# Nineteen second-pass pairs by seven products instead of fourteen, sums of their weights on GpSimd, ten units kept unrounded

## The chip, the cores and the metric

The kernel runs on one core of one Trainium2 chip. The metric is the device time of one execution in microseconds (us); the kernel before takes 2128.05 us in the median of three runs (2127.59 to 2128.74). The engines of the core work side by side, each through its own queue in order: TensorE (PE, matrix products), VectorE (DVE), ScalarE (ACT), GpSimd (POOL) and SyncE (SP, whose queue issues most loads). GpSimd's queue also issues loads and stores.

## What is computed

Two layers of a decoder, 256 tokens by 2048 features, all in float32. The part that the change touches is the second half of each layer:

```python
hm = _rmsnorm(x, mlp_norm_g[l]) @ w_up[l]          # 256x2048 by 2048x8192
x = x + jnp.square(jax.nn.relu(hm)) @ w_down[l]    # 256x8192 by 8192x2048
```

A float32 product is made of three products of rounded operands: each operand is split into hi (rounded) and lo (the rest), and hi*hi, hi*lo and lo*hi are added up (TERMS). ScalarE writes hi as a rounded copy, VectorE writes lo as a subtraction, source minus hi.

## The kernel before

The 8192 hidden features are worked through as 32 **pairs** of 128 features (NP = 32). A pair's activations are a block of two by two (two halves of the tokens, two groups of features), and so is a half of its rows of w_down: two groups of 128 rows by two column chunks of 512 (CH).

- **First pass** (`for i in range(NP)`, from line 1176): the up projection of pair i (L1124, results named upc), its square (`square`, L1137), and, two pairs later (LAG = 2), the product with the left 1024 columns of w_down, by seven products in place of eight block products (L1172, results named pr). The seven products need sums of the activations (S1 to S4, a **unit** h of eight 128x128 blocks, VectorE in `square`) and sums of the weights (t, four 128x512 blocks). `rounded` (L1161) splits a unit into hi and lo (f). The units are stored to DRAM for the second pass: as all seven rounded blocks (`whole`, 896 KB) for pairs that go by seven again, as four rounded blocks (`plain`) for the others. L1250 then does the left columns of the last two pairs.
- **Second pass** (`for i in ORDER`, L1274): the right 1024 columns of w_down, in the order 30, 31, 0, 1, ..., 29 (ORDER). Results are named rt. Fourteen pairs (SEVEN: every second one from the fourth on) go by seven products: seven times three terms, 21 matmuls of 128x512 (L1172 again). The other eighteen (ORDINARY) go by eight block products, 24 matmuls (L1337; the last at L1322). Their activations come back from DRAM through GpSimd's queue (`load_unit`, L1078): f for a seven, g (two pairs a block, `block`) for an ordinary one.
- **Weights** are made by jobs. An ordinary pair has two: a raw tile is loaded, and each of its halves is split into whi and wlo (L325 on ScalarE, L326 on VectorE, 128x1024). A seven has three (`quarters`, L989): plain (b1 of 128x512 and b2 of 128x1024), sums (t13) and more (t24), each split by L998 (ScalarE) and L999 (VectorE). The sums themselves are three VectorE operations: t[0:2] of 128x1024 (L1016), t[2] and t[3] of 128x512 (L1019, L1020). `weights.take` makes jobs three ahead of the one that TensorE uses (AHEAD = 3); in the second pass a table (`weights.order`) spreads a seven's three jobs between those of the ordinary pairs ahead of it.
- **Order**: TensorE's instructions are in program order. A scheduler orders the other engines' instructions, except that those marked `late` keep their program order, and those issued within `behind(x)` come after x. Tiles of a pool share buffers: an instruction that writes a tile waits until the buffer's last user is done.

Each layer begins with the mixer (attention, gated convolution, output projection, whose results are named q, k, v, gc, ci, gb, o). GpSimd does some elementwise work there, such as scaling the gate (L841) and the convolution's result (L736), and the small factors of the norms (L501, L708, L711).

Of the kernel before, what the change touches and what calls it, by code (L numbers as in the profile page):

```python
# [15 lines left out]
P = 128  # L16
# [96 lines left out]
def trunk(ctx: ExitStack, tc: tile.TileContext, x, w_in, w_out, conv_w, q_norm_g, k_norm_g,  # L113
# [5 lines left out]
    xpool = ctx.enter_context(tc.tile_pool(name="xpool", bufs=1))  # L119
    apool = ctx.enter_context(tc.tile_pool(name="apool", bufs=4))  # L120
    wpool = ctx.enter_context(tc.tile_pool(name="wpool", bufs=3))
# [382 lines left out]
    class Norm:  # L504
# [3 lines left out]
        def __init__(self, which, l):  # L508
            self.which, self.l = which, l
            self.squared = 0  # L510
            self.tiles = [Parts(apool, "a", f"nT{which}{l}_{n}") for n in range(D // CH)]
            self.ss = small.tile([P, NT, D // CH], F32, tag="ss", name=f"ss{which}{l}", bufs=2)
# [253 lines left out]
    def mixer(l, norm, loads):  # L766

        with ExitStack() as scope:
# [23 lines left out]

            def part_rooms():
                return (apool.tile([P, 2, 2 * CH], F32, tag="a", name="oraw"),
                        apool.tile([P, 4, CH], F32, tag="a", name="ot"))

            load_seven = {}
            for i in SIDE:
                if i in SIDE_SEVEN:
                    load_seven[i] = weights.seven(  # L800
                        w_out[l], 2 * P * i, bias_room if i == SIDE_SEVEN[0] else part_rooms,
                        spare2)
# [130 lines left out]
    def mlp(l, mnorm, ahead, last):  # L933
# [3 lines left out]
        with ExitStack() as scope:  # L937
            upool = scope.enter_context(tc.tile_pool(name="upool", bufs=3))
            fpool = scope.enter_context(tc.tile_pool(name="fpool", bufs=2))
# [21 lines left out]
            def column(i, c, kh):  # L961
                def make():
                    if c == 0:
                        raws[kh] = upool.tile([P, 8, 2 * P], F32, tag="uraw", name="uraw")
# [12 lines left out]
                weights.jobs.append(make)  # L977

            def load_rows(i, col):
                raw = (upool.tile([P, 2, 2 * CH], F32, tag="uraw", name="raw") if col and i not in SEVEN else  # L980
                       tile_of("draw", [P, 2, 2 * CH], F32, (first, "draw"), (second, "draw1"),
                               (second, "draw2")))
# [6 lines left out]
            def quarters(i, col=0):  # L989


                keep = late if i == SEVEN[0] and col else lambda ins: None

                def parts(src, tag, bufs):
                    hi, lo = (tile_of(tag + p, list(src.shape), F32R,
                                      *((r, tag + p) for r in (quarter if tag[0] == "b" else halves, second)[:bufs]))
                              for p in "hl")
                    keep(nc.scalar.activation(hi, src, AF.Copy))  # L998
                    keep(nc.vector.tensor_sub(lo, src, hi.bitcast(F32)))  # L999
                    return hi, lo  # L1000

                def load():
                    forms["raw"] = load_rows(i, col).rearrange("p k (n c) -> p k n c", n=2)
                    return forms["raw"]

                def plain():
                    raw = forms["raw"] if i == col == 0 else load()
                    h1, l1 = parts(raw[:, 0, 0], "b1", 2)
# [3 lines left out]
                def sums():  # L1012
                    raw = forms["raw"]
                    t = forms["t"] = first.tile([P, 4, CH], F32, tag="t", name="t")

                    keep(nc.vector.tensor_sub(t[:, 0:2], raw[:, :, 1], raw[:, 0]))  # L1016
                    h, lw = parts(t[:, 0:2], "t13", 1)

                    keep(nc.vector.tensor_add(t[:, 2], t[:, 1], raw[:, 0, 0]))  # L1019
                    keep(nc.vector.tensor_sub(t[:, 3], raw[:, 1, 0], t[:, 2]))  # L1020
                    return (h[:, 0], lw[:, 0]), (h[:, 1], lw[:, 1])
# [4 lines left out]

                if i == 0 and col == 0:
                    made = {}
# [4 lines left out]
                    return tuple(lambda n=n: made[n] for n in range(3))  # L1033
                if i == 1 and not col:

# [5 lines left out]
                    return tuple(behind_last(make) for make in (plain, sums, more))  # L1041
                return plain, sums, more

            def rows(i, k, box, col=0):
# [19 lines left out]
            for i in range(NP - LAG, NP):  # L1064
# [5 lines left out]

            whole = {i: dram.tile([P, 2, 7, P], F32R, name=f"whole{l}_{i}") for i in SEVEN}
            plain = [dram.tile([P, 2, 2, 4, P], F32R, name=f"plain{l}_{b}")
                     for b in range(len(PLAIN) // 2)]
            again, unit_loads = {}, []

            def load_unit(dst, src):
                with behind(*unit_loads[-1:]):
                    unit_loads.append(nc.gpsimd.dma_start(dst, src))  # L1078

            def load_again(i):  # L1080
                again[i] = fpool.tile([P, 2, 8, P], F32R, tag="f", name="f")
                load_unit(again[i][:, :, 1:], whole[i])

            base = len(weights.jobs)
            where = {}
            for i in ORDER:
                where[i] = len(weights.jobs)
                if i in SEVEN:
                    weights.jobs += quarters(i, 2 * CH)
# [4 lines left out]
            made_in = list(range(base))  # L1094
            mine = [where[i] + k for i in ORDINARY for k in range(2)]
            slots = {}
            for i in SEVEN:
                before = [j for j in mine if j < where[i]][-4:] if i != SEVEN[0] else [
                    mine[0], mine[1], mine[4]]
                js = [where[i] + k for k in range(3)]  # L1100
                if len(before) == 4 and SEVEN.index(i) and where[SEVEN[SEVEN.index(i) - 1]] > before[0]:
                    before = [before[2], before[2], before[3]]
                for j, b in zip(js, before):
                    slots.setdefault(b, []).append(j)
            for j in mine:
                made_in.append(j)
                made_in += slots.get(j, [])
            weights.order = made_in

# [27 lines left out]
            def square(i, h):  # L1137
# [8 lines left out]
                if i < NP - LAG:  # L1146
# [73 lines left out]
            def block(b):  # L1220
                blocks[b] = apool.tile([P, 2, 2, 4, P], F32R, tag="a", name="g")
                for s in range(2):
                    load_unit(blocks[b][:, s], plain[b][:, s])
# [48 lines left out]
            for n in (5, 4, 8):  # L1272
                prods[n] = bank(f"rt{l}{n}")
            for i in ORDER:  # L1274
                if i in SEVEN:
# [27 lines left out]
                n = ORDINARY.index(i)  # L1303
                if NP // 2 - 6 <= n and sums:
                    finish_left()
                if 0 < n <= len(SEVEN):
                    load_again(SEVEN[n - 1])
                b, slot = divmod(n - LAG, 2)
# [79 lines left out]
```

## Time and profile before

| what | before |
|---|---|
| median of three runs | 2128.05 us (2127.59 to 2128.74) |
| the profiled execution, whole | 2129.09 us |
| its span, first to last instruction | 2127.1 us |
| granted TensorE clock | 1.00 throughout |
| up projection and first pass, layer 0 | about 392 to 902 us |
| second pass, layer 0 | 902.2 to 1067.6 us |
| up projection and first pass, layer 1 | about 1448 to 1958 us |
| ScalarE, VectorE, GpSimd busy | 61%, 81%, 9% of the span |

In the profile's rows L12 is line 12 of the kernel, "out<-in" names the tiles, "xcount" the number of instructions, and an arrow "<-" behind an idle time names what ended the wait. "Busy" time of an engine includes time that an instruction spends held up after it has started. Matmul durations overlap, so TensorE's rate is read from the chain of waits, whose pieces follow one another.

### The profile page before, as it was taken

Reading aid. Unit: us, or ns where it says so; the run is one execution under the profiler, and the core shown is the slowest. Engines: PE = TensorE matmul, PEld = TensorE weight load, DVE = VectorE, ACT = ScalarE, POOL = GpSimd, SP = SyncE. Lnnn points to the kernel's source line nnn. Section 1 sums busy time; section 2 is a strip of 40 time slices with the busy share of each in tenths; the row PEclk is TensorE's granted clock in tenths of the full one; section 3 lists DMA queues with packets and bytes.
Section 4 is the critical chain, followed back from the end, with each engine's and each line's share of the span. In section 5 each row is a group of like instructions: output and inputs, shape, how many; then the busy total and the mean of one; then the engine's idle time right before and its main releaser. Section 6 shows DMA issues by size and latency. Waiting matters only on the chain.

```text
span 2127.1 us, 28890 instructions
## 1 busy us (share of the span) xinstructions
PE 2121.4 (100%) x10932; PEld 1806.0 (85%) x10932; DVE 1727.1 (81%) x2379; ACT 1295.3 (61%) x1771; POOL 188.9 (9%) x282
## 2 busy tenths in 40 slices
PE   9999999999999999999999999999999999999999
PEld 7888888888888888888888888888888888888887
DVE  6677678788888888799866776887888888887897
ACT  6556456666666666555565664566666666665553
POOL 2021200000000000011011221000000000000110
PEclk9999999999999999999999999999999999999999
DMA  7655567687777777699666556676778778786994
GB/s 249 199 159 168 179 218 244 205 253 243 241 246 243 242 246 243 215 363 345 224 210 178 159 167 192 212 249 218 239 245 250 236 245 250 236 246 209 385 357 158
DMA packets 293322, 497.99 MB, mean 234 GB/s; under 512 B 10723, under 2 KB 191541, under 8 KB 293184
## 3 DMA queue, kind: packets, MB, share of 16 engines
q1 hardware_dynamic: 263056, 406.88, 60.0%
q0 software_dynamic: 30080, 89.26, 13.0%
q8 instruction: 85, 1.39, 0.3%
q14 instruction: 53, 0.43, 0.1%
q10 hardware_dynamic: 48, 0.02, 0.0%
HBM read 451.53 MB, written 44.59 MB: 233 GB/s over the span
## 4 chain that ended last, share of the span: by engine, by line
PE 99%; DVE 0%; DMA 0%; ACT 0%; issue 0%
PE upc L1124 31%; PE pr L1172 14%; PE rt L1337 8%; PE rt L1172 6%; PE ci L479 4%; PE gc L479 4%; PE gb L479 4%; PE q L457 4%; PE k L457 4%; PE v L457 4%; PE o L457 4%; PE o L875 3%; PE o L893 1%; PE upw L1124 1%; PE up L1124 1%; PE pr L1250 1%
## 5 line engine op out<-in xcount | busy, mean ns | idle before, releaser
L325 ACT ACTIVATE whi<-raw 128x1024 fp32r<-128x1024 f32 x308 | 326.4, 1060 | 407.9 <-PE rt L1337 138.7
L326 DVE TENSOR_TENSOR wlo<-raw,whi 128x1024 fp32r<-128x1024 f32 x308 | 378.6, 1231 | 196.6 <-ACT whi L325 191.6
L1124 PE MATMUL upc<-nT,uhi 128*128 128x512 f32 x1920 | 477.5, 391 | 0.0
L974 ACT ACTIVATE uhi<-uraw 128x1024 fp32r<-128x1024 f32 x256 | 270.5, 1057 | 262.9 <-PE upc L1124 238.6
L975 DVE TENSOR_TENSOR ulo<-uraw,uhi 128x1024 fp32r<-128x1024 f32 x256 | 313.0, 1223 | 123.5 <-ACT uhi L974 113.8
L1124 PEld LDWEIGHTS upc<-nT,uhi 128*128 128x128 f32 x1920 | 352.7, 188 | 68.2
L1124 PEld LDWEIGHTS upc<-nT,ulo 128*128 128x128 f32 x1920 | 261.9, 190 | 18.7
L1124 PE MATMUL upc<-nT,ulo 128*128 128x256 f32 x1920 | 267.7, 282 | 0.0
L1337 PE MATMUL rt<-whi,g 128*128 128x512 f32 x480 | 152.8, 389 | 0.0
L999 DVE TENSOR_TENSOR t13l<-t,t13h 128x1024 fp32r<-128x1024 f32 x88 | 107.5, 1222 | 1.8
L1016 DVE TENSOR_TENSOR t<-draw 128x1024 f32<-128x1024 f32 x88 | 107.3, 1220 | 0.8
L999 DVE TENSOR_TENSOR t24l<-t,t24h 128x1024 fp32r<-128x1024 f32 x88 | 107.1, 1217 | 0.0
L999 DVE TENSOR_TENSOR b2l<-draw,b2h 128x1024 fp32r<-128x1024 f32 x88 | 107.1, 1217 | 0.0
L1337 PEld LDWEIGHTS rt<-whi,g 128*128 128x128 f32 x480 | 90.1, 188 | 18.6
L998 ACT ACTIVATE t13h<-t 128x1024 fp32r<-128x1024 f32 x88 | 93.4, 1061 | 3.0 <-PE rt L1172 0.6
L1172 PE MATMUL pr<-t13h,f 128*128 128x512 f32 x240 | 93.8, 391 | 0.0
L1337 PE MATMUL rt<-wlo,g 128*128 128x512 f32 x240 | 93.4, 389 | 0.0
L998 ACT ACTIVATE b2h<-draw 128x1024 fp32r<-128x1024 f32 x88 | 92.4, 1050 | 0.9 <-PE pr L1172 0.8
L998 ACT ACTIVATE t24h<-t 128x1024 fp32r<-128x1024 f32 x88 | 92.7, 1053 | 0.2
L457 PE MATMUL k<-whi,nT 128*128 128x512 f32 x256 | 86.1, 400 | 0.0
L457 PE MATMUL q<-whi,nT 128*128 128x512 f32 x256 | 84.8, 401 | 0.0
L457 PE MATMUL v<-whi,nT 128*128 128x512 f32 x256 | 84.1, 396 | 0.0
(414 smaller groups left out, 4097.2 us busy)
## 6 DMA issues: line engine op xcount, KB each, us to landing
uraw<-in_w_up_dram SPq DMA_DIRECT2D x128, 1024.0 KB, 5.8
raw<-in_w_in_dram SPq DMA_DIRECT2D x190, 512.0 KB, 4.1
draw<-in_w_down_dram SPq DMA_DIRECT2D x92, 1024.0 KB, 6.5
raw<-in_w_down_dram SPq DMA_DIRECT2D x36, 1024.0 KB, 8.2
raw<-in_w_out_dram SPq DMA_DIRECT2D x52, 512.0 KB, 4.6
whole<-f POOLq DMA_DIRECT2D x28, 896.0 KB, 4.5
f<-whole POOLq DMA_DIRECT2D x28, 896.0 KB, 8.6
plain<-f POOLq DMA_DIRECT2D x32, 512.0 KB, 3.7
```

What stands on the lines that cost most here:

```text
L325: self.splits.append((nc.scalar.activation(hi, raw, AF.Copy), nc.vector.tensor_sub(lo, raw, hi.bitcast(F32))))
L326: nc.vector.tensor_sub(lo, raw, hi.bitcast(F32))))
L457: nc.tensor.matmul(acc[:, t], a.ap[:, pa, k % KG, t * P:(t + 1) * P], (hi, lo)[pw][:, j], start=(k == 0 and n == 0), stop=(k == nk - 1 and ...
L479: nc.tensor.matmul(acc[:, f, 0] if part else acc[:, f], wt[:, k % 4, fs], a.ap[:, 0, k % KG] if part else a.ap[:, :, k % KG], start=(part ...
L974: nc.scalar.activation(hi, src, AF.Copy)
L975: nc.vector.tensor_sub(lo, src, hi.bitcast(F32))
L998: keep(nc.scalar.activation(hi, src, AF.Copy))
L999: keep(nc.vector.tensor_sub(lo, src, hi.bitcast(F32)))
L1016: keep(nc.vector.tensor_sub(t[:, 0:2], raw[:, :, 1], raw[:, 0]))
L1124: nc.tensor.matmul(acc[:, 0] if part else acc, wt[:, k], a.ap[:, 0, k % KG] if part else a.ap[:, :, k % KG], start=(part == 0 and kh == 0 ...
L1172: nc.tensor.matmul(prods[n], f[:, pa, a], b[pw], start=(start and m == 0), stop=(stop and m == 2))
L1337: nc.tensor.matmul(prods[p], own(k, t, pa), w[pw][:, n], start=(i == ORDER[0] and k == 0 and m == 0), stop=False)
```

## The change

Nineteen pairs of the second pass go by seven products: in positions 3, 4, 6, 7, 9, 10, ... 27, 28 of ORDER, and 29. Thirteen stay ordinary. A steady piece of the second pass is now ordinary, seven, seven.

Ten of the nineteen (KEPT: those whose position is not divisible by three) have their unit stored as four unrounded blocks in place of seven rounded ones. In the second pass the four come back, GpSimd makes S1 to S4 again (`unit_again`, four operations of 128x128, L1147), and ScalarE and VectorE round the unit again (L1217, L1218, 128x896).

The weights' sums of the second pass are now three GpSimd operations (`right_sums`, L1065 to L1067) made two pairs ahead, marked `late`; the loads are issued three pairs ahead (`right_load`). The splits are L1075 (ScalarE) and L1076 (VectorE), into forms that take turns over five rooms (`form_room`). The table of the second pass's jobs is gone: jobs are made in ORDER, three ahead. The pools apool and upool give each tile a buffer of its own name. In the first pass the sums stay on VectorE.

```diff
-SEVEN = ORDER[3:NP - LAG:2]
+SEVEN = tuple(i for p, i in enumerate(ORDER[:NP - LAG]) if p > LAG and p % 3 < 2 or p == NP - LAG - 1)
+KEPT = tuple(i for p, i in enumerate(ORDER) if i in SEVEN and p % 3)
...
+            def right_sums(n):
+                if n >= len(SEVEN):
+                    return
+                raw = raws[n, "r"]
+                t = raws[n, "t"] = tile_of("t", [P, 4, CH], F32, (upool, "u2"), (first, "t"))
+                late(nc.gpsimd.tensor_tensor(t[:, 0:2], raw[:, :, 1], raw[:, 0], op=ALU.subtract))
+                late(nc.gpsimd.tensor_tensor(t[:, 2], t[:, 1], raw[:, 0, 0], op=ALU.add))
+                late(nc.gpsimd.tensor_tensor(t[:, 3], raw[:, 1, 0], t[:, 2], op=ALU.subtract))
...
+            def right_jobs(n):
...
+                def plain():
+                    raw = raws[n, "r"]
+                    b1 = parts(raw[:, 0, 0], [
+                        tile_of("b1" + p, [P, CH], F32R, (quarter, "b1" + p), (second, "b1" + p))
+                        for p in "hl"])
+                    h, lw = parts(raw[:, 1], form_room())
+                    return b1, (h[:, 0], lw[:, 0]), (h[:, 1], lw[:, 1])
...
+            def unit_again(n):
...
+                if i in KEPT:
+                    h = again[n, "h"]
+                    for dst, x, y, op in ((S1, A21, A22, ALU.add), (S2, S1, A11, ALU.subtract),
+                                          (S3, A11, A21, ALU.subtract), (S4, A12, S2, ALU.subtract)):
+                        late(nc.gpsimd.tensor_tensor(h[:, dst], h[:, x], h[:, y], op=op))
+                    again[i] = rounded(h, 1, 8)
+                else:
+                    again[i] = fpool.tile([P, 2, 8, P], F32R, tag="f", name="f")
+                    load_unit(again[i][:, :, 1:], whole[i])
...
                 if i in SEVEN:
+                    if i in KEPT:
+                        stored.append(nc.gpsimd.dma_start(kept[i], h[:, 0:4]))
                     f = rounded(h, 1, 8)
-                    nc.gpsimd.dma_start(whole[i], f[:, :, 1:])
+                    if i not in KEPT:
+                        nc.gpsimd.dma_start(whole[i], f[:, :, 1:])
...
                     product(4, f, A22, t4, False)
                     work.tick()
+                    n = SEVEN.index(i)
+                    right_load(n + 3)
+                    load_kept(n + 3)
+                    right_sums(n + 2)
+                    unit_again(n + 2)
```

GpSimd's queue in the middle of layer 0's second pass, first before the change (f and g are units loaded back; in brackets what a row waits for: PE, DVE, Pool and Activation are the engines, DMASW a transfer of GpSimd's queue, DMAHW one of SP's):

```order
L1078 DMA f<-whole_7_3825 128x2x896 [waits DMASW7_49,DMASW1_49,PE_49]
L1078 DMA f<-whole_9_3826 128x2x896 [waits DMASW4_49,PE_49]
L1078 DMA g<-plain_3_3839 128x1024
L1078 DMA g<-plain_3_3839 128x1024 [waits DMASW2_49]
L1078 DMA f<-whole_11_3827 128x2x896 [waits DMASW7_49,DMASW3_49,PE_49]
```

And the same place with the change, one period of three pairs (t are sums of weights, h the unit of a kept pair, draw the raw weights):

```order
L1131 DMA h<-kept_8_3833 128x512
L1065 TENSOR_TENSOR t<-draw 128x1024 [waits DMAHW6_49,DVE_49]
L1066 TENSOR_TENSOR t<-t,draw 128x512 [waits Pool_49]
L1067 TENSOR_TENSOR t<-draw,t 128x512 [waits Pool_49]
L1131 DMA f<-whole_7_3824 128x2x896 [waits DMASW5_49,PE_49]
L1065 TENSOR_TENSOR t<-draw 128x1024 [waits DMAHW0_49,DVE_49]
L1066 TENSOR_TENSOR t<-t,draw 128x512 [waits Pool_49]
L1067 TENSOR_TENSOR t<-draw,t 128x512 [waits Pool_49]
L1147 TENSOR_TENSOR h<-h 128x128 [waits DMASW0_49]
L1147 TENSOR_TENSOR h<-h 128x128 [waits Pool_49]
L1147 TENSOR_TENSOR h<-h 128x128
L1147 TENSOR_TENSOR h<-h 128x128 [waits Pool_49]
```

Loads alone have become loads with ten elementwise operations between them in each period; the load of a rounded unit (f) waits for TensorE and stands ahead of the second pair's sums.

VectorE's queue in layer 0's second pass before the change, one ordinary pair and one seven (wlo, t24l, b1l, b2l and t13l are lo parts, t the sums):

```order
L326 TENSOR_TENSOR wlo<-raw,whi 128x1024
L999 TENSOR_TENSOR t24l<-t,t24h 128x1024
L999 TENSOR_TENSOR b1l<-draw,b1h 128x512
L999 TENSOR_TENSOR b2l<-draw,b2h 128x1024
L999 TENSOR_TENSOR t13l<-t,t13h 128x1024
L1016 TENSOR_TENSOR t<-draw 128x1024
L1019 TENSOR_TENSOR t<-t,draw 128x512
L326 TENSOR_TENSOR wlo<-raw,whi 128x1024
L1020 TENSOR_TENSOR t<-draw,t 128x512
```

With the change, one ordinary pair and two sevens (wfl and wf are lo parts of the forms, f a kept unit's lo part, x an addition of results):

```order
L327 TENSOR_TENSOR wlo<-raw,whi 128x1024
L1320 TENSOR_TENSOR x_83<-x_83,e_8501 128x512
L1218 TENSOR_TENSOR f<-h,f 128x896
L327 TENSOR_TENSOR wlo<-raw,whi 128x1024
L1076 TENSOR_TENSOR b1l<-draw,b1h 128x512
L1076 TENSOR_TENSOR wfl<-t,wfh 128x1024
L1076 TENSOR_TENSOR wfl<-draw,wfh 128x1024
L1076 TENSOR_TENSOR wfl<-t,wfh 128x1024
L1076 TENSOR_TENSOR b1l<-draw,b1h 128x512
L1076 TENSOR_TENSOR wfl<-t,wfh 128x1024
L1076 TENSOR_TENSOR wf<-draw,wf 128x1024
L1076 TENSOR_TENSOR wfl<-t,wfh 128x1024
```

The three sums have left VectorE's queue, and the rounding of a kept unit has come in.

More of the change, by code (lines that the diff above doesn't have):

```diff
@@ L979, in load_rows @@
             def load_rows(i, col):
-                raw = (upool.tile([P, 2, 2 * CH], F32, tag="uraw", name="raw") if col and i not in SEVEN else
+                raw = (tile_of("raw", [P, 2, 2 * CH], F32, (upool, "u0"), (upool, "u1"))
+                       if col and i not in SEVEN else
                        tile_of("draw", [P, 2, 2 * CH], F32, (first, "draw"), (second, "draw1"),
@@ L987, in load_rows, with quarters @@
                 return raw
-            def quarters(i, col=0):
-                keep = late if i == SEVEN[0] and col else lambda ins: None
+            def quarters(i):
                 def parts(src, tag, bufs):
@@ L1067, in mlp @@
                 rows(i, 1, box)
-            whole = {i: dram.tile([P, 2, 7, P], F32R, name=f"whole{l}_{i}") for i in SEVEN}
+            whole = {i: dram.tile([P, 2, 7, P], F32R, name=f"whole{l}_{i}")
+                     for i in SEVEN if i not in KEPT}
+            kept = {i: dram.tile([P, 4, P], F32, name=f"kept{l}_{i}") for i in KEPT}
             plain = [dram.tile([P, 2, 2, 4, P], F32R, name=f"plain{l}_{b}")
-                     for b in range(len(PLAIN) // 2)]
+                     for b in range((len(PLAIN) + 1) // 2)]
             again, unit_loads = {}, []
@@ L1078, in load_unit, with load_kept @@
                     unit_loads.append(nc.gpsimd.dma_start(dst, src))
[L1080 to L1085, printed above, removed]
+                late(unit_loads[-1])
+            def load_kept(n):
+                if n < len(SEVEN) and SEVEN[n] in KEPT:
+                    h = again[n, "h"] = tile_of("h", [P, 8, P], F32, (fpool, "h"), (second, "h"))
+                    load_unit(h[:, 0:4], kept[SEVEN[n]])
+            def unit_again(n):
+                if n >= len(SEVEN):
+                    return
+                i = SEVEN[n]
+                if i in KEPT:
[7 more added lines that the diff above has]
+                    load_unit(again[i][:, :, 1:], whole[i])
             for i in ORDER:
-                where[i] = len(weights.jobs)
                 if i in SEVEN:
-                    weights.jobs += quarters(i, 2 * CH)
+                    weights.jobs += right_jobs(SEVEN.index(i))
                 else:
@@ L1093, in mlp @@
                     rows(i, 1, box, 2 * CH)
[L1094 to L1108, printed above, removed]
             def column_bank():
@@ L1273, in mlp @@
                 prods[n] = bank(f"rt{l}{n}")
+            for n in range(3):
+                right_load(n)
             for i in ORDER:
```

73 lines of the change are left out of this document (51 added, 22 removed).

## The prediction

> **What bounds the kernel now.** I read the page first, then the chain of waits at the first layer's second pass, then the stages, then VectorE's and GpSimd's groups, then single overlaps in the timeline.
>
> ```profile
> span 2127.1 us, 28890 instructions
> PE 2121.4 (100%) x10932; PEld 1806.0 (85%) x10932; DVE 1727.1 (81%) x2379; ACT 1295.3 (61%) x1771; POOL 188.9 (9%) x282
> PE 99%; DVE 0%; DMA 0%; ACT 0%; issue 0%
> ```
>
> TensorE is busy throughout and is 99% of the chain that ended last. So a matmul removed is time gained, as long as nothing else becomes late. GpSimd, at 9%, looks free.
>
> ```profile
> 883.65 5.56 PE upc L1124 x32
> 889.21 2.07 PE pr L1172 x9
> 891.28 10.88 PE pr L1250 x48
> 902.16 16.32 PE rt L1337 x72
> 918.48 4.76 PE rt L1172 x21
> 923.24 5.44 PE rt L1337 x24
> ...
> 1062.17 5.44 PE rt L1322 x24
> ```
>
> This is the chain (start, length, what) around the second pass of layer 0. L1337 is an ordinary pair, L1172 a pair by seven products. A pair of 24 matmuls takes 5.44 us, one of 21 takes 4.76: 0.2267 us per matmul. The pass runs without a gap from 902.16 to 1062.17 + 5.44 = 1067.61 us. Layer 1 repeats it.
>
> ```profile
> core 0: us, PE busy (x) PEld busy (x) DVE busy (x) ACT busy (x) POOL busy (x), PEclk, DMA share, GB/s
> 891.00:1069.00 178.00, 178.00 (x799) 147.67 (x798) 155.32 (x166) 97.61 (x117) 17.60 (x28) 1.00 0.83 294
> ```
>
> In that stage VectorE is busy 155.3 of 178 us, and GpSimd does nothing but issue 28 loads. VectorE is the next bound there; the change takes work from it and gives it to GpSimd.
>
> **What is removed.** Five more pairs per layer go from 24 to 21 matmuls: 5 x 3 x 2 = 30 matmuls, 30 x 0.2267 = 6.80 us. If everything else stays hidden, the profiled execution goes from 2129.09 (its span of 2127.1 and 2.0 around it) to 2122.29 us. The median of the runs is 2128.05, 1.04 under the profiled one, so that case is 2121.2.
>
> **What VectorE has to do per period.** In the steady part three pairs repeat: one ordinary, one seven with a stored rounded unit, one seven with a kept unit. TensorE needs 66 x 0.2267 = 14.96 us for them.
>
> ```profile
> L326 DVE TENSOR_TENSOR wlo<-raw,whi 128x1024 fp32r<-128x1024 f32 x37 | 45.2, 1224 | 18.0 <-ACT whi L325 17.9
> L1016 DVE TENSOR_TENSOR t<-draw 128x1024 f32<-128x1024 f32 x14 | 17.1, 1223 | 0.4
> L999 DVE TENSOR_TENSOR b1l<-draw,b1h 128x512 fp32r<-128x512 f32 x14 | 9.6, 685 | 0.0
> L1019 DVE TENSOR_TENSOR t<-t,draw 128x512 f32<-128x512 f32 x14 | 9.6, 688 | 0.3
> ```
>
> These are groups of the same stage (busy us, mean ns). An ordinary pair has two lo parts of 128x1024 (L326): 2.44 us. A seven has three of them and a 128x512 one: 3 x 1.22 + 0.69 = 4.35 us. The sums (1.22 + 2 x 0.69 = 2.60 us a pair, L1016 to L1020) leave VectorE. A kept unit adds one rounding of 128x896, by elements 7/8 of 1.22 = 1.07 us. Sum: 2.44 + 2 x 4.35 + 1.07 = 12.2 us. That is under 14.96: alone, VectorE would have become more comfortable than it was. ScalarE makes the hi parts to the same shapes; priced like VectorE's they are 5 x (4.35 - 2.44) + 10 x 1.07 = 20 us more on top of its 98 of 178 us, so it has room.
>
> **What GpSimd has to do per period.**
>
> ```profile
> L841 POOL TENSOR_TENSOR gc02w<-gc02w,rowb 128x512 f32<-128x512 f32 x1 | 1.3, 1287 | 0.0
> L708 POOL TENSOR_TENSOR ams<-ams,rc x32: 195/197/654, 111.5 to 1281.2; 128x2 f32<-128x2 f32 x32
> L1078 POOL DMA_DIRECT2D f<-whole x14 | 10.0, 712 | 131.3 <-PE rt L1172 106.2 <-PE rt L1337 25.1
> L1078 POOL DMA_DIRECT2D g<-plain x14 | 7.7, 551 | 0.0
> ```
>
> A 128x512 operation took 1.29 us, a 128x2 one 0.195 us (shortest and median). The 128x1024 one of the change does not occur in this trace: at most two of 512, 2.58 us; at least twice the 1.15 us that a 512 one takes once it runs (below), 2.30 us. A 128x128 one lies between a quarter of 1.15 (0.29) and the line through the two rows (0.47). Sums of a pair: 4.60 to 5.16 us. Sums of a kept unit, four operations: 1.16 to 1.88. Per period 2 x 4.60 + 1.16 = 10.4 to 12.2 us, and about three DMA issues of 0.55 to 0.71. GpSimd alone would fit into 14.96, if barely. The Trainium skill ("GPSIMD Engine Reference", Performance versus the Vector engine) gives 4497 ns for 2048 elements; an estimate from it is 2.25 us for 1024, and the sum of a pair would be 4.55 us. No run here shows that size yet.
>
> **Where the two meet.** The timeline of the mixer stage shows GpSimd beside VectorE:
>
> ```profile
> 226.49 1.29 POOL L841 TENSOR_TENSOR gc02w<-gc02w,rowb 128x512 f32<-128x512 f32 x1
> 226.70 2.15 DVE L326 TENSOR_TENSOR wlo<-raw,whi 128x1024 fp32r<-128x1024 f32 x1 [0.97 <-ACT whi L325]
> 227.73 1.18 POOL L711 TENSOR_TENSOR af<-a_r,rc 128x2 f32<-128x2 f32 x1
> ...
> 1319.20 1.22 DVE L326 TENSOR_TENSOR wlo<-raw,whi 128x1024 fp32r<-128x1024 f32 x1
> 1319.30 2.27 POOL L736 TENSOR_TENSOR cv<-cv,rowb 128x512 f32<-128x512 f32 x1 [13.72 <-ACT whi L325]
> ...
> 248.37 1.29 POOL L841 TENSOR_TENSOR gc03w<-gc03w,rowb 128x512 f32<-128x512 f32 x1 [5.06 <-DVE gc03w L493]
> 249.26 1.49 DVE L326 TENSOR_TENSOR wlo<-raw,whi 128x1024 fp32r<-128x1024 f32 x1 [0.97 <-ACT whi L325]
> ...
> 200.68 1.29 POOL L841 TENSOR_TENSOR gc01w<-gc01w,rowb 128x512 f32<-128x512 f32 x1
> 201.22 0.56 DVE L686 TENSOR_TENSOR pT<-ptp,pT 128x384 fp32r<-128x384 f32 x1 [1.30 <-ACT pT L685]
> ```
>
> VectorE's subtraction that started at 226.70 took 2.15 us, not 1.22: it ended 1.07 us after GpSimd's operation did (226.49 + 1.29 = 227.78). The tiny GpSimd operation behind it, worth 0.2, took 1.18 and ended with VectorE's, at 228.9. At 1319.30 GpSimd took 2.27, ending 1.15 us after VectorE's end. At 249.26 VectorE ended 1.09 us after GpSimd. In each of these cases one waited for the whole of the other. At 201.22 a VectorE operation with one source in PSUM (ptp) ran beside GpSimd at its usual 0.56. So two operands in SBUF on both sides exclude each other. All the VectorE work counted above (L327, L1076 and L1218 of the changed kernel) and all the GpSimd sums are of that kind.
>
> Two pages of the Trainium skill disagree on this. "Advanced Engine Details and Errata", VectorE Performance Modes, names interference only for VectorE instructions that run in a two-port mode; by it fp32 subtractions would run beside the sums, and the result would be the 2121.2 us above. "SBUF — State Buffer", Who interferes with whom, says that a VectorE instruction with two SBUF inputs contends with a GpSimd one that reads SBUF, and that the later one blocks fully. The trace agrees with the second (2.15 us against 1.22).
>
> **The sum with exclusion.** Waiting hides an instruction's start, so a 1024 one then costs 1.07 to 1.09 us of exclusive time (the two cases above); I take 1.08, and with it 0.54 for 512 and 0.95 for 896. VectorE per period: 2 x 1.08 + 2 x (3 x 1.08 + 0.54) + 0.95 = 10.7 us at the low end, 12.2 at the high one. With GpSimd's 10.4 to 12.2 that is 21.1 to 24.4 us in a period for which TensorE needs 14.96. TensorE would starve 6 to 9 us in every period.
>
> For a whole layer: VectorE has 19 sevens (71.8 to 82.7), about ten ordinary pairs' parts inside the congested stretch (21.6 to 24.4), ten roundings (9.5 to 10.7), four additions L1320 of 512 (2.2 to 2.8): 105 to 121 us (the ends unrounded: 105.1 and 120.6). GpSimd has 19 sums (87.4 to 98.0) and ten units (11.6 to 18.8): 99.0 to 116.8. Together 204 to 237 us. The stretch starts when GpSimd's first sum can: its queue has a load of block 0 ahead, into a tile that the up projection reads until 889.2, so about 890. It ends with the last form of the nineteenth seven; behind that TensorE still has that pair's last 6 matmuls and two ordinary pairs, 54 x 0.2267 = 12.2 us. The pass would end at 890 + 204 + 12 = 1106 to 890 + 237 + 12 = 1139, instead of 1067.6 - 3.4 = 1064.2. That is 42 to 75 us a layer.
>
> Within this I take 69 us. The two ends' middle is 59; but nobody uses the exclusive time when VectorE's next instruction waits for ScalarE or for GpSimd's sum, and it already waits 18 us for ScalarE in this stage (the L326 row above). Half of that, 9 to 10 us, is added. So 2122.29 + 2 x 69 = 2260.3 in the profiled execution, **2259 us** as a median: 6% slower.
>
> **What else moves.** The first pass stores kept units (128x512) in place of rounded ones and rounds as before; the next user of such a unit's buffer comes two pairs later, with four pieces like the chain's first row above (5.56 us each, 22 us) in between, and a store of three and a half times the size lands in 4.5 us. I cost it at nothing.
>
> ```profile
> draw<-in_w_down_dram SPq DMA_DIRECT2D x92, 1024.0 KB, 6.5
> ...
> whole<-f POOLq DMA_DIRECT2D x28, 896.0 KB, 4.5
> f<-whole POOLq DMA_DIRECT2D x28, 896.0 KB, 8.6
> ```
>
> The sevens' right-hand weights are issued on SP's queue three pairs ahead, one before the sums need them, and took 6.5 us to land; a pair lasts 4.8 us in TensorE's time and 7 in the forecast's, so they are nearly or wholly hidden, and a remainder would show as GpSimd waiting for a load while VectorE uses the time. The kept units' loads stand equally far ahead of their sums. Both at nothing; if the exclusion is not there, a late load costs at most 6.5 - 4.8 = 1.7 us a pair, and only where the forms made ahead run out.
>
> **Rivals.**
> 1. *No exclusion in this stage, or it overlaps.* Then 2121.2, 0.3% faster. Place: the steady period. TensorE stays the bound if VectorE's 10.7 us and the part of GpSimd's 10.4 that excludes it fit into 14.96: that is, if under 4.3 us, some 40%, of the sums' time really excludes. For it: VectorE and GpSimd alone both fit. Against it: every overlap above is whole. Chance 6%.
> 2. *Half the sums' time excludes* (say, only one of the two engines waits): 10.7 to 12.2 plus 5.2 to 6.1 is 15.9 to 18.3 us a period, 1 to 3 over, about nine periods a layer: 2121 + 18 to 54, about 2155. Against it: both engines were seen waiting. Chance 7%.
> 3. *The queues add to it.* On GpSimd the load of a stored unit waits for TensorE to leave its buffer and stands ahead of the next sums; VectorE, in order, stands at the roundings that need GpSimd's unit sums. If TensorE's lateness holds GpSimd and that holds VectorE for another 2 to 3 us in each of the nine periods, 2 x 9 x 2.5 = 45 us come on top: 2300. For it: GpSimd already waits 131 us at those loads (the f<-whole row). Chance 10%.
> 4. *The change does not do what it says*: ruled out by the instruction order, which has 30 matmuls fewer and the sums on GpSimd.
>
> **How the numbers follow.** The forecast has the remaining 77%. Its bounds are 2121.2 + 84 = 2205 and 2121.2 + 150 = 2271; the range reaches on to 2300 for most of rival 3, and leaves out rivals 1 and 2. 0.2% (4 us) is about what a measurement can tell from no change. Faster 6% (rival 1), same 2%, slower 92%.
>
> **What would show it.** Right: in the second passes TensorE has gaps of 6 to 9 us per three pairs, released by VectorE's lo parts; means of L1076 and L327 there rise far over 1.22 and 0.69 us, and those of GpSimd's sums over 2.6 and 1.3; busy time of both then includes waiting. First pass and mixer keep their lengths. Wrong: L1076 stays at 1.22 beside GpSimd's sums, or TensorE's second pass stays at 162 us.

## The result and the profile after

The changed kernel takes **2253.56 us** (median of five runs, 2252.85 to 2254.24), the kernel before 2128.05 (2127.59 to 2128.97) beside it: a ratio of 1.0589 with a 95% interval of 1.0574 to 1.0604. It is 5.9% slower; 2259 with a range of 2205 to 2300 was forecast. The profiled execution took 2252.85 us, its span is 2250.9. These are its totals, and the chain of work that ended last by engine:

```profile
span 2250.9 us, 29148 instructions
PE 2155.6 (96%) x10902; PEld 1817.4 (81%) x10902; DVE 1867.9 (83%) x2335; ACT 1328.6 (59%) x1811; POOL 552.5 (25%) x476
PE 81%; DVE 8%; POOL 5%; issue 4%; ACT 1%; DMA 0%; POOLq 0%; DVEq 0%; ACTq 0%
```

TensorE has its 30 matmuls fewer (10932 to 10902) and is now 81% of the chain, no longer 99%. The stages of layer 0 (busy us of each engine, then the granted clock) say where; the first line is the first pass, the second the second pass, the last two are single periods of three pairs within it:

```profile
core 0: us, PE busy (x) PEld busy (x) DVE busy (x) ACT busy (x) POOL busy (x), PEclk, DMA share, GB/s
413.00:891.00 478.00, 478.00 (x2551) 413.23 (x2551) 413.68 (x556) 317.35 (x385) 25.78 (x35) 1.00 0.75 232
902.00:1128.00 226.00, 182.34 (x723) 142.96 (x722) 214.47 (x136) 108.20 (x127) 186.31 (x118) 0.89 0.61 208
972.82:995.74 22.92, 19.50 (x73) 14.84 (x71) 22.45 (x13) 10.92 (x13) 21.44 (x15) 0.88 0.72 237
995.74:1017.59 21.85, 17.40 (x67) 13.32 (x67) 21.38 (x13) 9.95 (x12) 20.34 (x13) 0.92 0.58 198
```

TensorE still fills the first pass. In the second it is busy 182 of 226 us, while VectorE and GpSimd are both "busy" nearly all of a period of 22 to 23 us. Much of that is waiting, as the groups of the same stage show (busy us, then mean ns of one):

```profile
L1076 DVE TENSOR_TENSOR wfl<-t,wfh 128x1024 fp32r<-128x1024 f32 x31 | 63.8, 2059 | 1.8 <-ACT wfh L1075 1.8
L327 DVE TENSOR_TENSOR wlo<-raw,whi 128x1024 fp32r<-128x1024 f32 x28 | 45.8, 1646 | 3.9 <-ACT whi L326 3.9
L1218 DVE TENSOR_TENSOR f<-h,f 128x896 fp32r<-128x896 f32 x10 | 27.6, 2764 | 1.4 <-ACT f L1217 1.4
...
L1065 POOL TENSOR_TENSOR t<-draw 128x1024 f32<-128x1024 f32 x19 | 58.8, 3096 | 11.9 <-DVE wfl L1076 9.4 <-DMA draw<-in_w_down_dram 1.3 <-DVE wf L1076 1.1
L1147 POOL TENSOR_TENSOR h<-h 128x128 f32<-128x128 f32 x40 | 51.6, 1309 | 0.8
```

Subtractions of 128x1024 took 1.22 us before; in these two groups they take 1.65 and 2.06. A GpSimd sum of 128x1024 takes 3.10 in the mean. A piece of the timeline shows one period's worst place:

```profile
986.68 3.91 DVE L1218 TENSOR_TENSOR f<-h,f 128x896 fp32r<-128x896 f32 x1 [0.47 <-ACT f L1217]
987.26 2.37 POOL L1065 TENSOR_TENSOR t<-draw 128x1024 f32<-128x1024 f32 x1
990.64 0.50 PE L1226 MATMUL rt<-b1h,f 128*128 128x512 f32 x1 [3.21 <-DVE f L1218]
...
996.70 3.42 DVE L1076 TENSOR_TENSOR wfl<-t,wfh 128x1024 fp32r<-128x1024 f32 x1
999.12 2.16 POOL L1066 TENSOR_TENSOR t<-t,draw 128x512 f32<-128x512 f32 x1
1000.05 1.78 DVE L1076 TENSOR_TENSOR b1l<-draw,b1h 128x512 fp32r<-128x512 f32 x1
1001.36 1.62 POOL L1067 TENSOR_TENSOR t<-draw,t 128x512 f32<-128x512 f32 x1
```

The rounding at 986.68 ended 0.96 us after GpSimd's sum did (987.26 + 2.37 = 989.63), though it had started first; TensorE stood 3.21 us for it. From 996.70 on the two engines take turns, each waiting for the other's operation in hand. TensorE's waits in this second pass, by what ended them (us in total, times, longest):

```profile
PE rt L1226 <- DVE f L1218: 26.9, 9, 6.1
PE rt L1226 <- ACT f L1217: 14.1, 7, 3.4
PE rt L1226 <- DVE wfl L1076: 2.6, 2, 2.2
```

### The profile page after: what moved, and what is told of

It is laid out like the page before. It is cut to its first block, busy times and chain, and to the rows that moved or that the text cites. A ratio compares the mean times of both kernels' runs of the same rounds, so it can differ in the third digit from the quotient of the medians.

```text
span 2250.9 us, 29148 instructions
## 1 busy us (share of the span) xinstructions
PE 2155.6 (96%) x10902; PEld 1817.4 (81%) x10902; DVE 1867.9 (83%) x2335; ACT 1328.6 (59%) x1811; POOL 552.5 (25%) x476
## 4 chain that ended last, share of the span: by engine, by line
PE 81%; DVE 8%; POOL 5%; issue 4%; ACT 1%; DMA 0%; POOLq 0%; DVEq 0%; ACTq 0%
PE upc L1175 30%; PE pr L1226 13%; PE ci L480 4%; PE gc L480 4%; PE gb L480 4%; PE k L458 4%; PE v L458 4%; PE q L458 4%; PE o L458 4%; DVE wfl L1076 3%; PE o L877 2%; POOL t L1065 2%; POOL h L1147 2%; DVE wlo L327 2%; DVE b1l L1076 1%
## 5 line engine op out<-in xcount | busy, mean ns | idle before, releaser
L327 DVE TENSOR_TENSOR wlo<-raw,whi 128x1024 fp32r<-128x1024 f32 x288 | 375.1, 1307 | 167.4 <-ACT whi L326 162.5
L326 ACT ACTIVATE whi<-raw 128x1024 fp32r<-128x1024 f32 x288 | 304.5, 1059 | 313.3 <-PE ci L480 40.5
L977 DVE TENSOR_TENSOR ulo<-uraw,uhi 128x1024 fp32r<-128x1024 f32 x256 | 313.1, 1223 | 123.8 <-ACT uhi L976 113.5
L1226 PE MATMUL rt<-wfh,f 128*128 128x512 f32 x368 | 137.1, 437 | 0.0
L1218 DVE TENSOR_TENSOR f<-h,f 128x896 fp32r<-128x896 f32 (+2 forms) x84 | 128.9, 1535 | 5.9 <-ACT f L1217 5.9
L1076 DVE TENSOR_TENSOR wfl<-t,wfh 128x1024 fp32r<-128x1024 f32 x62 | 126.1, 2037 | 5.7 <-ACT wfh L1075 5.7
L1217 ACT ACTIVATE f<-h 128x896 fp32r<-128x896 f32 (+2 forms) x84 | 80.6, 960 | 84.1 <-POOL h L1147 83.1
L1065 POOL TENSOR_TENSOR t<-draw 128x1024 f32<-128x1024 f32 x38 | 120.8, 3178 | 23.6 <-DVE wfl L1076 18.4
L1226 PE MATMUL rt<-b1h,f 128*128 128x512 f32 x76 | 37.2, 490 | 83.6 <-DVE f L1218 50.9
L1147 POOL TENSOR_TENSOR h<-h 128x128 f32<-128x128 f32 x80 | 103.3, 1310 | 1.6
L1401 PE MATMUL rt<-whi,g 128*128 128x512 f32 x320 | 102.1, 390 | 0.0
L1075 ACT ACTIVATE wfh<-t 128x1024 fp32r<-128x1024 f32 x62 | 65.0, 1051 | 58.3 <-PE rt L1226 21.9
L1226 PEld LDWEIGHTS rt<-wfh,f 128*128 128x128 f32 x368 | 80.7, 219 | 18.1
```

The costliest lines, as they stand in the source:

```text
L326: self.splits.append((nc.scalar.activation(hi, raw, AF.Copy), nc.vector.tensor_sub(lo, raw, hi.bitcast(F32))))
L327: nc.vector.tensor_sub(lo, raw, hi.bitcast(F32))))
L1065: late(nc.gpsimd.tensor_tensor(t[:, 0:2], raw[:, :, 1], raw[:, 0], op=ALU.subtract))
L1147: late(nc.gpsimd.tensor_tensor(h[:, dst], h[:, x], h[:, y], op=op))
L1218: nc.vector.tensor_sub(f[:, 1, lo:hi], h[:, lo:hi], f[:, 0, lo:hi].bitcast(F32))
L1226: nc.tensor.matmul(prods[n], f[:, pa, a], b[pw], start=(start and m == 0), stop=(stop and m == 2))
```

## The experiments

Each kernel has one run beside runs of the kernel before on the same chip (their medians are 2127.5 to 2129.2 us), unless more are named.

**Do GpSimd's operands in SBUF slow VectorE at all?** Three kernels leave the kernel before as it is and add four GpSimd operations of 128x512 per ordinary pair of the second pass, whose result nobody reads. The first, *two operands*:

```diff
+                for _ in range(4):
+                    late(nc.gpsimd.tensor_tensor(
+                        idle.rearrange("p (a c) -> p a c", c=P), ones.unsqueeze(1).to_broadcast([P, 4, P]),
+                        ident.unsqueeze(1).to_broadcast([P, 4, P]), op=ALU.add))
```

> The kernel before, with four GpSimd additions of 128x512 (two SBUF operands) beside each of the 18 ordinary second-pass pairs of a layer, written to a tile that nobody reads. Nothing waits for them. Theory (a two-operand GpSimd operation and a two-operand VectorE operation in SBUF exclude each other): 72 x 1.15 = 83 us of exclusive time a layer beside VectorE's some 125 in a pass of 165, so TensorE starves some 40 us a layer: 2190 to 2230 us. Rival (the time after the change comes from the new chain GpSimd, ScalarE, VectorE, TensorE, whose links wait for each other): no chain here, 2128 us.

In the second, *none*, the loop's body is `late(nc.gpsimd.memset(idle, 0.0))`:

> As the run before, but the four GpSimd instructions are memsets of 128x512: they write and read nothing. Theory, if it is the reading that excludes: VectorE's subtractions keep 1.22 us and the time stays 2128 us. Rival (any GpSimd instruction that is running holds VectorE): VectorE's subtractions beside them grow as in the run before, and the time by the memsets' own length.

In the third, *one*, it is a `tensor_scalar` of `ones` alone (times 0.5, plus 1.0):

> As the run with four unread GpSimd additions beside each ordinary pair in the kernel before, but with one SBUF operand (tensor_scalar of 128x512) in place of two. Theory, if one read is enough to exclude: VectorE's subtractions beside them grow beyond 1.22 us and the time rises by the shorter operations' length, above 2150 us. Rival (it takes two operands on GpSimd's side): 2128 us, as with memsets.

Measured: two operands **2243.3 us** (above the 2190 to 2230 expected), one operand **2148.85**, none **2127.52**. Layer 0's groups, the added operation and a lo part of VectorE for each kernel in this order:

```profile
L1310 POOL TENSOR_TENSOR idle<-ones,ident 128x512 f32<-128x512 f32 x72 | 131.8, 1830 | 4.4
L326 DVE TENSOR_TENSOR wlo<-raw,whi 128x1024 fp32r<-128x1024 f32 x34 | 58.8, 1734 | 0.0
```
```profile
L1310 POOL TENSOR_SCALAR idle<-ones 128x512 f32<-128x512 f32 x72 | 88.2, 1225 | 4.8
L999 DVE TENSOR_TENSOR b2l<-draw,b2h 128x1024 fp32r<-128x1024 f32 x14 | 22.0, 1568 | 0.0
```
```profile
L1310 POOL MEMSET idle<- 128x512 f32 x72 | 38.3, 532 | 2.9
L326 DVE TENSOR_TENSOR wlo<-raw,whi 128x1024 fp32r<-128x1024 f32 x38 | 46.4, 1225 | 17.7 <-ACT whi L325 17.6
```

An operation without a source in SBUF leaves VectorE at 1.22 us and the time where it was; one source already costs 20 us in the whole (just under the 2150 named), two cost 116. Work that nobody waits for makes the kernel slower: no wait on its results can be the reason. The 116 us are above what was expected, most likely because queues in order pass the delay on, which the expectation had not counted. These are ScalarE's waits and TensorE's in the second pass of the kernel with two operands:

```profile
ACT t24h L998 <- DVE t L1020: 98.7, 14, 10.8
```
```profile
PE rt L1172 <- DVE b2l L999: 36.2, 9, 5.7
```

VectorE's own delayed sums (L1020) hold ScalarE, and the lo parts behind hold TensorE.

**Is it the reading, or the new order and loads?** In the changed kernel all GpSimd sums become memsets of the same tiles; weights' sums and kept units' sums are left out of what is computed, the queues, buffers, loads and waits stay.

```diff
-                late(nc.gpsimd.tensor_tensor(t[:, 0:2], raw[:, :, 1], raw[:, 0], op=ALU.subtract))
+                late(nc.gpsimd.memset(t[:, 0:2], 0.0))
...
-                        late(nc.gpsimd.tensor_tensor(h[:, dst], h[:, x], h[:, y], op=op))
+                        late(nc.gpsimd.memset(h[:, dst], 0.0))
```

> The changed kernel with the weights' sums and the kept units' sums left out: GpSimd writes zeros in their place with memsets of the same shapes, in the same order, and all that waits for them still does. Theory (reading excludes): VectorE back at 1.22 us for 1024, 12.2 us of work in a period of 14.96, time 2121 us, or up to 2126 where a chain is late. Rival (the chain over GpSimd and ScalarE costs the time): the chain is shorter by what a memset is shorter than a sum, but stays; well above 2128 us.

Measured: **2120.98 us**, and VectorE's group is at its old length:

```profile
L1065 POOL MEMSET t<- 128x1024 f32 x19 | 18.5, 972 | 10.5 <-DVE wfl L1076 10.0 <-DVE wf L1076 0.5
L1076 DVE TENSOR_TENSOR wfl<-t,wfh 128x1024 fp32r<-128x1024 f32 x31 | 37.7, 1222 | 4.2 <-ACT wfh L1075 4.2
```

That is the 2121.2 of the first rival to a fraction of a microsecond: the matmuls give their 6.8 us, the rest of the change is hidden, and with the sums left out the time is 133 us less. (A memset is also shorter than a sum, 0.97 against 2.37 us; in the kernels with added work above nobody waits for the result, and beside memsets VectorE's operations kept their 1.22 us, so there it was not the length.)

**Which sums?** Four kernels move them apart. All sums on VectorE (`nc.vector` in place of `nc.gpsimd` in both places; `late` stays on the weights' sums of the first two sevens alone, so the scheduler may place the others, here and in every kernel below with sums on VectorE):

> The changed kernel with all its new GpSimd operations (weights' sums and kept units' sums) issued on VectorE instead: the same operations, the same results waited for, one engine fewer. Theory (on two engines they run one after the other anyway, and each costs VectorE less than GpSimd): per period 2 x 1.14 + 2 x (4.03 + 2.36) + 1.01 + 0.8 = 16.9 us on VectorE, 2 over TensorE's 14.96, nine periods, two layers: 2121 + 35 = about 2156 us, range 2140 to 2180. Rival (the chain of sums, rounding and splitting, or the nineteen sevens and their kept units, cost the time): VectorE now has the work of both, so no faster than 2250 us.

Measured: **2168.05 us**, 12 above the expectation's centre. VectorE's 128x128 operation was 0.285 us there, and it was busy 181.7 of the stage's 188 us: it is the bound, by its own work.

No kept unit (`KEPT = ()`), weights' sums on GpSimd as in the change:

> The changed kernel without kept units: all nineteen units are stored and loaded rounded; the weights' sums stay on GpSimd. Theory: exclusive time per period is VectorE's 10.7 - 0.95 = 9.7 and GpSimd's 9.2, 18.9 us in place of 21.0 (both by the low prices), 2.1 us less in nine periods and two layers: 2253 - 40 = 2213 us, range 2190 to 2230. Rival (the kept units' new chain, GpSimd's four sums, ScalarE's and VectorE's rounding, costs most of the time): below 2150 us.

Measured: **2204.07 us**, in the range. With the weights' sums alone on GpSimd the time is 83 us over the 2121 without reading sums (that kernel had the kept units as well).

Kept units' sums on GpSimd, weights' sums left out (memsets):

> The changed kernel with the weights' sums left out (GpSimd writes zeros in their place) and the kept units' sums left in. Theory (a two-operand GpSimd operation gets in when VectorE pauses or its turn comes; VectorE, with 12.2 us in 14.96, pauses in each period): 2121 to 2130 us. Rival (each chain of four small sums costs 5 to 10 us wherever it stands, as it did where VectorE also made the weights' sums): above 2150 us.

Measured: **2123.26 us**: the kept units' sums alone cost about 2 us. VectorE has pauses there (busy 133.7 of the 158 us from 902 to 1060), and 78 of the 80 sums got in after at most the one VectorE operation in hand.

Kept units' sums on GpSimd, weights' sums on VectorE:

> The changed kernel with only the weights' sums moved to VectorE; the kept units' four small sums stay on GpSimd. Theory: per period VectorE 10.7 + 2 x 2.2 = 15.1, GpSimd 4 x 0.33 = 1.3, together 16.4 us in 14.96: 2121 + 9 x 2 x 1.4 = about 2147 us, range 2135 to 2175. Rival (the kept units' chain costs most): stays above 2200 us.

Measured: **2191.35 us**. This was a miss, 44 above. The whole trace has these GpSimd operations (shortest, median and longest ns), and the timeline shows one of the long ones with the first three and the last of the VectorE operations beside it, and the rounding that needs it:

```profile
L1148 POOL TENSOR_TENSOR h<-h x80: 454/474/10748, 907.0 to 2157.7; 128x128 f32<-128x128 f32 x80
```
```profile
963.02 0.68 DVE L1077 TENSOR_TENSOR b1l<-draw,b1h 128x512 fp32r<-128x512 f32 x1
963.62 1.22 DVE L1077 TENSOR_TENSOR wfl<-t,wfh 128x1024 fp32r<-128x1024 f32 x1
964.76 0.68 DVE L1067 TENSOR_TENSOR t<-t,draw 128x512 f32<-128x512 f32 x1
...
969.97 1.22 DVE L1077 TENSOR_TENSOR wfl<-draw,wfh 128x1024 fp32r<-128x1024 f32 x1
973.90 1.09 DVE L1219 TENSOR_TENSOR f<-h,f 128x896 fp32r<-128x896 f32 x1 [2.71 <-ACT f L1218]
```
```profile
962.79 8.73 POOL h L1148
```
```profile
L1219 DVE TENSOR_TENSOR f<-h,f 128x896 fp32r<-128x896 f32 x10 | 10.9, 1090 | 20.8 <-ACT f L1218 20.8
```

A GpSimd operation of 0.45 us began at 962.79 and ended at 971.52, when nine VectorE operations back to back, each at its unhindered length, had passed it. VectorE then came to the rounding of that very unit (L1219) and stood still, until all four sums and ScalarE's hi part were made one after the other. It stood 20.8 us per layer there, where the expectation had counted some 13 for the sums of ten units (1.3 each): that is 16 of the 44 us in two layers. By an estimate, most of the rest is VectorE's own price: back to back its operations start 1.14 us (1024) and 0.60 us (512) apart in the rows above, while the expectation had 1.08 and 0.54. Sixteen of them in each of nine periods make 9 us a layer, and the pass's four additions, which it left out, 2.4 more. Against the kernel with the same sums on VectorE, 2168.05, their place on GpSimd costs 23 us. So the exclusion isn't a matter of turns alone; a stream without a pause can starve the other engine. In the changed kernel itself that was rare: counted in its trace, 188 of its 194 GpSimd sums got in after at most the one VectorE operation in hand, one let five and one eight pass; of the 80 here, 15 let two to eleven pass.

**What is the best without GpSimd's sums?** Four kernels take all sums to VectorE and keep every unit rounded. First nineteen sevens (no kept unit, and the weights' sums on VectorE), timed in six runs:

> Nineteen sevens, all units stored rounded (no kept ones), all sums on VectorE: GpSimd only issues loads. Theory: VectorE needs 2 x 1.14 + 2 x (3 x 1.14 + 0.61 + 1.14 + 2 x 0.61) = 15.1 us in a period in which TensorE needs 14.96, and has slack at both ends of the pass: 2121 to 2132 us, faster than the changed kernel by 5.5% and perhaps than the one before. Rival (nineteen sevens themselves, by their forms, rooms and loads, cost the time): stays above 2200 us.

Measured: **2133.83 us** (2132.45 to 2135.68), ratio 1.0030 (1.0017 to 1.0042): a miss, just above the 2121 to 2132 expected. TensorE's waits are 2.7 and 3.2 us in the two passes for loads of units, and 1.3 and 0.5 us for VectorE's parts; the loads come late. A third buffer for units, from the rooms that the kept ones left, with seventeen sevens (the edit in part; the sums are on VectorE too):

```diff
+SEVEN = tuple(i for p, i in enumerate(ORDER[:NP - LAG]) if p > LAG and p % 5 in (1, 3, 4))
+KEPT = ()
...
+                    if n % 3 == 2:
+                        again[i] = tuple(r.tile([P, 8, P], F32R, tag="h", name="f3", bufs=1) for r in (fpool, second))
...
-                    unit_again(n + 2)
+                    unit_again(n + 3)
```

> Seventeen sevens (of five pairs three: ordinary, seven, seven, ordinary, seven), all units rounded, all sums on VectorE, and a third buffer for loaded units, so that each is loaded two pairs ahead. Theory: VectorE needs 2 x 2.28 + 3 x 6.39 = 23.7 us per five pairs, TensorE 3 x 4.76 + 2 x 5.44 = 25.2; no GpSimd operation reads; the loads that were late in the run with nineteen are early: three pairs x 3 x 2 = 18 matmuls less, 2127.6 - 4.1 = 2123.5 us, range 2122 to 2127. Rival (VectorE's queue in order, with two sevens in a row, makes TensorE wait as in the run with nineteen): 2128 us or more.

Measured in eleven runs: **2129.49 us** (2127.88 to 2130.91), ratio 1.0007 (0.9998 to 1.0016), a miss. In layer 0 the chain has a unit's load that was issued only at 911.99, when a VectorE sum (L1067) had released it, and TensorE waits for it:

```profile
911.99 12.58 DMA f<-whole
```
```profile
PE rt L1233 <- DMA f<-whole: 2.8, 1, 2.8
```

The time is that of the rival, but its cause is not: TensorE waits 0.4 us for VectorE's parts in that pass.

The same third buffer with nineteen sevens:

> Nineteen sevens, all units rounded, all sums on VectorE, with the third buffer for loaded units. Theory: VectorE needs 15.1 us per three pairs, and 2.4 us more for the four additions in the pass, TensorE 14.96: VectorE is the bound by 1 to 5 us a layer, and only the late loads of the run without the third buffer go: 2123 to 2131 us. Rival (the loads were all that was late there): 2121 us.

Measured in eleven runs: **2130.63 us** (2129.38 to 2132.86), ratio 1.0016 (1.0007 to 1.0025): no gain from the two further sevens. Last, seventeen sevens with the first three units loaded one pair earlier (`if n < 3: unit_again(n)`), the first of them into the third buffer (`n % 3 == 0` in place of 2):

> The run with seventeen sevens, its first three units loaded one pair earlier each: the first into the buffer that is free when the pass begins. In that run the second unit was loaded from 912.0 to 924.6 us while TensorE waited for it. Theory: that wait goes, about 6 us in a layer, and 18 matmuls less remain as gain: 2123 us, range 2121 to 2127, faster than the kernel before. Rival (the transfer finds its time taken by other transfers wherever it stands): 2128 us or more.

Measured in eleven runs: **2126.15 us** (2124.95 to 2128.06) against 2127.48 for the kernel before beside it, ratio 0.9994 (0.9985 to 1.0003). The late load is gone; TensorE's largest wait in that second pass is 1.2 us:

```profile
PE rt L1233 <- DVE wf L1077: 1.2, 1, 1.2
```

The median is in the range expected and 1.3 us under the kernel before, but the interval includes no change, so the gain that was expected is not shown. The wait that went had been 2.8 us, not the 6 that the expectation named. None of the four is measurably faster than the kernel before; the best version found without GpSimd's sums equals it.

## Why the prediction was right, and where its sum was off

- **Matmuls removed, 6.80 us.** Confirmed: 2120.98 us with memsets in place of the sums, against 2121.2.
- **The two engines exclude each other.** Confirmed from both sides: unread sums slow the kernel before, and the change without reads loses nothing. Rivals 1 and 2 (2121.2 and 2155) fall with it. The prediction had spoken of two operands in SBUF on both sides; one on GpSimd's side is enough (2148.85, and 1.57 us against 1.22). Of the two rules of the Trainium skill that the prediction weighed, "SBUF — State Buffer", Who interferes with whom, is the one that the trace agrees with (1.73 us against 1.22 beside unread sums); interference for two-port modes alone ("Advanced Engine Details and Errata", VectorE Performance Modes) would have the kernel with two operands at 2127.5 us, not 2243.3.
- **The period, 21.1 to 24.4 us.** The chain of waits has the starts of three consecutive sums of the same kind, and with them two periods of 22.92 and 21.85 us:

```profile
972.82 3.31 POOL t L1065
...
995.74 3.32 POOL t L1065
...
1017.59 3.32 POOL t L1065
...
1122.38 5.44 PE rt L1386 x24
```

- **The prices.** GpSimd's 1024 sum, bounded at 2.30 to 2.58 us, took 2.37 where nothing was in its way (987.26 above); the 128x128 one, bounded at 0.29 to 0.47, 0.45.
- **The layer, +69 us.** This is the term that was mis-sized. The pass of layer 0 ends at 1122.38 + 5.44 = 1127.8 us, 63.6 after the 1064.2 of the sum. Its pieces: the first GpSimd sum starts at 886.3, not 890; the last rounding ends at 1111.4, so the congested stretch is 225 us; 16.4 are left behind it, not 12.2. The ends' middle for the stretch was 220; so of the 9 to 10 us added for VectorE's own waits 4 to 5 are needed. VectorE's waits did become shorter beside GpSimd's sums, from 17.9 us (L326 before) to 3.9 (L327 now); that what it waited for was mostly ready by the time it got through is the likely reason, not a tested one. An early start and a shorter stretch (4 and 5 us) and a longer tail (4 us) partly cancel, and where between the two ends the time would fall had been a choice: that the forecast came within 6 us is in part luck. Layer 1 repeats it: the whole span grew by 123.8 us, twice 61.9, where 131 had been forecast.
- **Rival 3 (queues, 45 us on top)** did not come with its price, but its mechanism is there. GpSimd's queue stood at a unit's load until TensorE was done once in each layer, at the start of the pass (layer 0's row is the first below). In layer 1 a weights' sum that let eight VectorE operations pass held the queue, the load of a unit behind it was issued only at 2050.35, and TensorE waited 7.2 us for that load; the prediction had put late loads at nothing:

```profile
POOL f L1131 <- PE rt L1401: 7.7, 1, 7.7
```
```profile
2035.48 11.32 POOL L1065 TENSOR_TENSOR t<-draw 128x1024 f32<-128x1024 f32 x1 [4.76 <-DVE wfl L1076]
...
2050.35 0.75 POOL L1131 DMA_DIRECT2D f<-whole  x1
```
```profile
PE rt L1226 <- DMA f<-whole: 7.2, 1, 7.2
```

- **A sign that was named wrongly.** TensorE's gaps were to be released by the weights' lo parts. They were released by the kept units' rounding: 26.9 + 14.1 us of 43.6 in layer 0 by L1218 and L1217, 2.6 by L1076. They are also shorter than the 6 to 9 us named, 4.8 in the mean of nine periods, as the slower clock below takes a part of each period's excess. The kept unit's sums are the last that GpSimd makes in a period, and their rounding the last that TensorE needs. So the order of the work, as far as it can be read from the queues, decided which wait showed; the sum of both engines' work set the length of the period.
- **What was not foreseen** is the granted clock, 0.89 in that second pass. TensorE was busy 182.3 us there with work that takes 162 at the full clock, so of the 63.6 us lost some 20 show as longer matmuls and 43.6 as waits. That is not 20 us more of cost: had the clock stayed, TensorE would have waited for the same parts that much longer, in so far as they set the pace. How much of the 20 would have been saved was not measured.

## What to carry to other kernels

An engine that is 9% busy is not free if its work and that of the engine that feeds the bound exclude each other, as GpSimd's and VectorE's operations with sources in SBUF did here: add the two engines' times in one period before moving work, and compare that sum, not each engine alone, with the bound. To test it, put unread operations beside the existing work, once with two sources, once with none. If small work must stay on GpSimd beside VectorE, see that VectorE has pauses: the same sums cost about 2 us where it had them, and where it had none 23 us more than on VectorE itself.

## What the runs showed of the hardware that was not expected

- The order of start does not decide alone who goes first: the 0.45 us operation above waited 8.7 us behind nine VectorE operations that began after it, and the rounding at 986.68 let a sum pass that began 0.58 us later, as eight other VectorE operations of that trace did (0.06 to 0.58 us). What decides was not found. The Trainium skill ("SBUF — State Buffer", Who interferes with whom) has the order of issue decide; these places disagree, if the starts in the profile are the order of issue.
- After TensorE's wait of 3.2 us its matmuls ran slower. The windows around and behind that wait have TensorE's busy time and matmuls first, and the granted clock third from the end; the last one is the slow stretch alone:

```profile
986.00:990.60 4.60, 1.23 (x5) 0.37 (x3) 4.13 (x3) 4.60 (x6) 4.51 (x5) 1.00 1.01 367
990.60:996.00 5.40, 5.36 (x15) 3.95 (x16) 5.40 (x4) 2.53 (x4) 4.24 (x4) 0.68 0.72 219
996.00:1002.40 6.40, 6.40 (x29) 5.25 (x28) 6.40 (x4) 2.59 (x3) 6.24 (x3) 1.00 0.85 296
991.94:995.36 3.42, 3.42 (x10) 2.57 (x8) 3.42 (x3) 1.06 (x1) 2.72 (x2) 0.50 0.54 199
```

Fifteen matmuls in 5.36 us are 0.36 us each, and 29 in 6.40 are 0.22. The Trainium skill ("TensorE: Matmul & The Clock Gate", The HAM clock gate) has half the clock after a window of about 3.4 us without work and the full one after as long a busy stretch; the trace agrees in the 0.50 and in the length of this slow stretch, 3.4 us. It does not agree on the wait: 3.2 us were enough here, and 2.25 us later in the same pass, where the clock had been 1.00 from 1085.00 to 1097.70:

```profile
1097.48 0.58 PE L1226 MATMUL rt<-b1h,f 128*128 128x512 f32 x1 [2.25 <-ACT f L1217]
```
```profile
1097.76:1098.60 0.84, 0.73 (x2) 0.02 (x1) 0.84 (x1) 0.62 (x1) 0.84 (x1) 0.50 0.00 0
```
